# One convolution tap on ScalarE, the whole output projection in high and low parts, and a ring of three for modulation weights

## The chip, the cores and the metric

The kernel runs on one core of a Trainium2 chip. The metric is device time in microseconds (us) of one execution. Engines are named as in the profile: PE is TensorE (matmuls; PEld its weight loads), DVE is VectorE, ACT is ScalarE, POOL is GpSimd, SP is SyncE, which issues nearly all DMAs.

## What is computed

A trunk of two layers on one sequence of 256 tokens of width 1024. Each layer is a half-step SwiGLU feed-forward block (hidden width 2816), a token mixer, and another half-step feed-forward block. Every sublayer gets an RMS-normalized input with a shift and a scale, and its output a gate; these come from a conditioning vector through `mod_w` (a 1024 x 9216 matrix per layer). The mixer of layer 0 is stick-breaking attention, that of layer 1 the RG-LRU block, which the change is in:

```python
def rglru_block(h, w_in, conv_w, conv_b, w_r, b_r, w_i, b_i, lam, w_out):
    gate, xb = jnp.split(h @ w_in, 2, axis=-1)          # width 1280 each
    xp = jnp.pad(xb, ((0, 0), (CONV_W - 1, 0), (0, 0)))  # CONV_W = 4
    xc = conv_b + xp[:, 0:S] * conv_w[0]
    for tap in range(1, CONV_W):
        xc = xc + xp[:, tap:tap + S] * conv_w[tap]
    r = sigmoid(xblk @ w_r + b_r); i = sigmoid(xblk @ w_i + b_i)   # ten blocks of 128
    log_a = -LRU_C * r * softplus(-lam)
    a = exp(log_a); b = sqrt(-expm1(2 * log_a)) * (i * xc)
    hs = scan over tokens of  h = a * h + b
    return (gelu(gate) * hs) @ w_out
```

## The kernel before

Activations lie transposed, features on the 128 partitions and the 256 tokens along the free axis. A float32 product is made of three fp32r matmuls: weight and activation are each split into a high part (rounded to fp32r) and a low part (the rest), and high x high, high x low and low x high are summed in PSUM (`Acc.group`, the matmul is L553). A few products use a plain float32 matmul instead (`group32`, L570, and the gates' matmul, L1116), which needs no split.

Weights come in pieces of 128 x 2048 (1 MB) into a ring of three buffers (`raw`), by DMAs on SP's queue (`dma`, L495). `load` splits each piece in two halves of 1024 columns: ScalarE writes the high part (`wh`, L525), VectorE the low part (`wl`, L528), each into a ring of seven halves.

The modulation matrix is not multiplied on TensorE. `mod_tile` loads one tile of 128 x 1024 (512 KB) into a ring of four buffers (`rawm`), and VectorE multiplies it with the conditioning vector and sums it along the row (L585). There are 128 such tiles in this ring, handed out by `hook` between the steps of the feed-forward blocks and the attention, at a rate per step, each load ordered behind a matmul. The ring also holds three pieces of the weights of the RG-LRU's gates (`wg`).

Operations are collected with their buffers, and a planner (`Program.schedule`) puts them in an order per engine before the kernel is built, from its own costs, latencies and due times and from what is free in each ring. Each engine then runs its list in order, and semaphores make it wait where the other engines are later than planned. So a change of one ring or one operation can move other instructions too.

In the RG-LRU block (`rglru`) the branch `xb` is projected in five double tiles. Each tile n of 128 features is copied out of PSUM into a buffer of 4 + 256 columns by ScalarE, and `conv` makes the four taps on VectorE: a `tensor_scalar` with the weight of the first tap and the bias (L1095) and three `scalar_tensor_tensor` (L1098). `gates` makes two float32 matmuls (L1116), two sigmoids and a tanh on ScalarE, and a product (L1127). TensorE then does the five double tiles of the gate projection, while `decay` (exponentials and squares on ScalarE, L1173 on VectorE), `scan` (square root on ScalarE, L1179 and the scans L1182 on VectorE) and `output` (gelu on ScalarE, the product L1189 on VectorE) are made for the five double tiles. Exponential, square root and gelu each need another table on ScalarE, so all of a kind are made behind one table load (L1310).

`down` makes the output projection in five chunks c of two feature tiles, for eight output tiles d. In the first chunk (`N32 = 1`) the operand is the float32 product itself and the weights are the float32 piece, in sixteen plain float32 matmuls (L570). For the other four `output` splits the product: a copy on ScalarE is the high part, L1195 on VectorE the low part; and their weights are split by `load`. At the end of a `down` the residual (L695) follows for each d, then the square for the next norm and the scaled input of the next sublayer in two parts (`scaled`, L648), whose first matmuls start before the norm is known (`up_first`). `kick_op` (L740) is a small matmul that is put behind the first step of some chunks.

Of the kernel before, what the change touches and what calls it, by code (L numbers as in the profile page):

```python
# [10 lines left out]
AF = mybir.ActivationFunctionType  # L11
ALU = mybir.AluOpType
# [3 lines left out]
T = 256  # L16
TX = T + 2
D = 1024
# [4 lines left out]
NR = DR // P  # L23
# [21 lines left out]
OFF_CW = OFF_FG + KD  # L45
OFF_CB = OFF_CW + 4 * NR
# [306 lines left out]
def c_act(n, psum=False, ptr=0):  # L353
    return (51.0 if psum else 93.0) + 0.8333 * n + 93.0 * ptr


def c_dve(n):
    return 68.0 + 1.042 * n
# [11 lines left out]
def trunk(ctx, tc, xT, cb, par, modw, gu0, gu, wdn, qk, wv, wo, win, wri, wout, out):  # L370
    nc = tc.nc
    act, dve, pe, pool, sp = nc.scalar, nc.vector, nc.tensor, nc.gpsimd, nc.sync
# [10 lines left out]
    def ring(name, n, cols, dt=F32, pl=const, pitch=0):  # L383
        if pitch:
            whole = pl.tile([P, n * pitch], dt, tag=name, name=name)
            tiles = [whole[:, i * pitch : i * pitch + cols] for i in range(n)]
        else:
            tiles = [pl.tile([P, cols], dt, tag=f"{name}{i}", name=f"{name}{i}") for i in range(n)]
        return Space(name, n, lambda at, _: tiles[at]), tiles

    banks, _ = ring("bank", 8, 512, pl=psum)
    banks.exclusive = True
    rawr, _ = ring("raw", 3, CH)
    modr, _ = ring("rawm", 4, D)
    whr, _ = ring("wh", 7, HALF, F32R)
    wlr, _ = ring("wl", 7, HALF, F32R)
    const.tile([P, HXPAD], F32, tag="pad0", name="pad0")
    hxr, _ = ring("hx", 20, TX, F32R, pitch=320)
    const.tile([P, HKPAD], F32, tag="pad2", name="pad2")
    hkr, _ = ring("hk", 2, T, F32R)  # L400
    sqr, _ = ring("sq", 2, T)
    ssqr, _ = ring("ssq", 2, T)
    rmsr, _ = ring("rms", 1, T)
    rstr, _ = ring("rst", 1, T)
    hpr, _ = ring("hpre", 3, T)
    bcr, _ = ring("bc", 4, 2)
    tr, _ = ring("tr", 2, T)
    sgr, _ = ring("sg", 3, T)
# [6 lines left out]
    def new_phase(r_cells, f_cells, dts=(F32R, F32)):  # L415
        k = len(phases)
        prev = phases[-1]["spaces"] if phases else ()
        ph = {"size": (r_cells, f_cells), "dts": dts}

        def view(which):  # L420
            def v(at, n):
                enter(k)
                return phase["tiles"][which][:, at * CELL : (at + n) * CELL]
            return v

        ph["spaces"] = tuple(
            Space(f"ph{k}{n}", c, view(i), prev) for i, (n, c) in enumerate((("r", r_cells), ("f", f_cells))))
        phases.append(ph)
        return ph["spaces"]
# [15 lines left out]
    def fixed(name, cols, dt=F32):  # L445
        return const.tile([P, cols], dt, tag=name, name=name)
# [4 lines left out]
    pars = Buf(ap=fixed("pars", NPAR))  # L451
# [30 lines left out]
    def col(off, n=1):  # L482
        return pars()[:, off : off + n]
# [16 lines left out]
    def A(o, i, f, n, r, w, table=None, psum=False, ptr=0, after=(), **kw):  # L500
        def fn():
            act.activation(o(), i(), f, **{k: (v() if callable(v) else v) for k, v in kw.items()})  # L502
        return pr.op("ACT", c_act(n, psum, ptr), fn, r, w, after, table)

    def V(fn, n, r, w, cost=None, ptr=0):
        return pr.op("DVE", cost or c_dve(n) + 62.0 * ptr, fn, r, w)
# [572 lines left out]


    def rglru(l, s, nxt):
        N32 = 1
        R, F = new_phase(8 * (NB - N32), 86)
        xc, rr, th, gt, sig, wg, firsts = {}, {}, {}, {}, [], {}, []

        def of(t, n):
            return t[n // 2], n % 2, slice((n % 2) * T, (n % 2 + 1) * T)

        def conv(n, evict):
            xb = Buf(xbr)  # L1090
            evict(n % 2, xb)
            if n % 2 == 0:
                xc[n // 2] = Buf(F, 4)
            c, e, cs = of(xc, n)
            V(lambda: dve.tensor_scalar(c()[:, cs], xb()[:, 1 : 1 + T], col(OFF_CW + n), col(OFF_CB + n), ALU.mult,  # L1095
                                        ALU.add), T, [xb, pars], [(c, e)], ptr=2)
            for tap in range(1, 4):
                V(lambda tap=tap: dve.scalar_tensor_tensor(c()[:, cs], xb()[:, 1 + tap : 1 + tap + T],  # L1098
                                                           col(OFF_CW + tap * NR + n), c()[:, cs], ALU.mult, ALU.add), T,
                  [xb, pars, (c, e)], [(c, e)], ptr=1)  # L1100
# [28 lines left out]
        def xb_proj(n2):  # L1129
            if n2 == 0:  # L1130
                firsts.append(up_first((l, s), [load(win[1, i], CH, f"xb{i}") for i in range(NFIRST)]))
            if n2 < NFIRST:
                ts = next(firsts[0])

                def evict(e, xb):
                    t, rd, c = ts[e]
                    A(lambda: xb()[:, 4:], t, AF.Identity, T, [t, rd], [xb], ptr=1, bias=c)
            else:
                acc = Acc(f"xb{n2}")
                up(acc, load(win[1, n2], CH, f"xb{n2}"), (l, s), True)  # L1140

                def evict(e, xb):
                    A(lambda: xb()[:, 4:], lambda: acc.b()[:, e * T : (e + 1) * T], AF.Copy, T, [(acc.b, (e, 0))], [xb],
                      psum=True)
            for e in range(2):
                conv(2 * n2 + e, evict)
# [38 lines left out]
        def output(n2):  # L1185
# [3 lines left out]
            V(lambda: dve.tensor_tensor(t(), t(), g(), ALU.mult), 2 * T, tt + [g], tt)  # L1189
            if n2 < N32:  # L1190
                y = t
# [13 lines left out]
        for n2 in range(NB):  # L1205
            output(n2)
        down(l, s, nxt, [wout[:, 2 * c : 2 * c + 2, :].rearrange("p k d -> p (k d)") for c in range(NB)],
             lambda k: ys[k], 2, n32=N32, kicks=(N32,))

# [89 lines left out]
    ffn(0, 2, (1, 0), hook(2))  # L1299
    ffn(1, 0, (1, 1), hook(3))  # L1300
    rglru(1, 1, (1, 2))
    assert not todo
    ffn(1, 2, "end", lambda f: None)
# [62 lines left out]
```

## Time and profile before

| what | us |
|---|---|
| median of three runs (lowest, highest) | 962.55 (962.23, 963.67) |
| the profiled execution | 962.91 |
| its span, first to last instruction | 961.2 |
| TensorE busy in it | 949.2 |
| VectorE busy | 791.8 |
| ScalarE busy | 570.1 |
| the sixteen plain float32 products of the output projection (L570) | 7.2 |
| the first taps on VectorE (L1095, ten) | 4.1 |
| the modulation products in the ring (L585, 128) | 155.6 |

A line of a timeline has the start and the length in us, the engine, the line of the kernel, the operation, what it writes and reads, and in brackets the idle time before it and what ended that. A line of the groups has the count, the busy time in us, the mean ns of one and the idle time before. A line of a table by stretches has the stretch, then busy us and count for PE, PEld, DVE, ACT and POOL, then the granted clock of TensorE, the busy share of the DMA engines and GB/s. A line of waits has who waited for whom: us in total, times, longest us. A plain float32 matmul shows as two records.

### The profile page before, as it was taken

How to read it: one execution, taken by the hardware profiler on the slowest of the kernel's cores; microseconds unless marked ns; L12 is line 12 of the kernel's file. 1: busy time of each engine (PE TensorE's matmuls, PEld its weight loads, DVE VectorE, ACT ScalarE, POOL GpSimd, SP SyncE). 2: the span in 40 equal slices, each digit the busy share in tenths (PEclk: the TensorE clock that was granted, in tenths of full speed). 3: DMA queues.
4: the chain of work that ended last, by engine and by line, in shares of the span. 5: the costliest groups of instructions: out<-in, count | busy, mean ns of one | idle time of the engine just before them, and what ended most of it. 6: DMA issues, size and time to landing. Idle time of an engine off the chain costs nothing.

```text
span 961.2 us, 19726 instructions
## 1 busy us (share of the span) xinstructions
PE 949.2 (99%) x8132; PEld 936.2 (97%) x8132; DVE 791.8 (82%) x1291; ACT 570.1 (59%) x928; POOL 2.4 (0%) x15
## 2 busy tenths in 40 slices
PE   8999999999999999999999999999999999999996
PEld 6999999999999999999999999999999999999996
DVE  7899989798999999999799998855997996555443
ACT  6685544378886854454466545534879785445333
POOL 1000000000000000000000000000000000000000
PEclk9999999999999999999999999999999999999998
DMA  9979999945666489999976998965243746545531
GB/s 345 405 293 376 355 347 366 363 158 193 244 215 225 174 320 359 357 349 352 350 282 243 342 344 317 351 244 209 88 166 143 264 160 238 208 184 193 172 119 44
DMA packets 48044, 251.25 MB, mean 261 GB/s; under 512 B 5457, under 2 KB 6097, under 8 KB 28242
## 3 DMA queue, kind: packets, MB, share of 16 engines
q1 hardware_dynamic: 47378, 249.43, 69.8%
q8 instruction: 63, 1.03, 0.4%
q10 hardware_dynamic: 576, 0.56, 0.2%
q14 instruction: 27, 0.22, 0.1%
HBM read 248.92 MB, written 1.05 MB: 260 GB/s over the span
## 4 chain that ended last, share of the span: by engine, by line
PE 80%; DVE 8%; DMA 7%; ACT 3%; issue 2%; SPq 0%; DVEq 0%; ACTq 0%
PE bank L553 73%; DMA rawm<-in_modw 5%; DVE wl L528 2%; PE bank L919 2%; DVE arenaf L1098 1%; DMA raw<-in_gu 1%; PE bank L1042 1%; ACT arenaf L502 1%; PE bank L570 1%; ACT wh L525 1%; DVE rawm L585 1%; PE bank L630 1%; PE bank L995 1%; PE bank L1020 1%; DVE arenar L585 0%
## 5 line engine op out<-in xcount | busy, mean ns | idle before, releaser
L553 PE MATMUL bank<-hx,wh 128*128 128x256 f32 (+1 forms) x3236 | 560.5, 278 | 1.8 <-DVE hx L832 1.3
L525 ACT ACTIVATE wh<-raw 128x1024 fp32r<-128x1024 f32 (+1 forms) x328 | 336.2, 1046 | 282.1 <-PE bank L553 204.3
L553 PEld LDWEIGHTS bank<-hx,wh 128*128 128x128 f32 x3236 | 490.1, 188 | 3.8 <-DVE hx L832 1.8
L528 DVE TENSOR_TENSOR wl<-raw,wh 128x1024 fp32r<-128x1024 f32 (+1 forms) x328 | 389.2, 1208 | 105.4 <-ACT wh L525 104.9
L553 PE MATMUL bank<-hx,wl 128*128 128x256 f32 (+1 forms) x1618 | 448.0, 277 | 0.1
L553 PEld LDWEIGHTS bank<-hx,wl 128*128 128x128 f32 x1618 | 304.3, 188 | 0.3 <-DVE wl L528 0.3
L553 PE MATMUL bank<-arenar,wh 128*128 128x256 f32 x1664 | 285.0, 277 | 0.0
L553 PEld LDWEIGHTS bank<-arenar,wh 128*128 128x128 f32 x1664 | 250.6, 188 | 0.1
L553 PE MATMUL bank<-arenar,wl 128*128 128x256 f32 x832 | 229.7, 276 | 0.0
L585 DVE SCALAR_TENSOR_TENSOR rawm<-rawm,cact 128x1024 f32<-128x1024 f32 x128 | 155.6, 1220 | 20.8 <-DMA rawm<-in_modw 20.0
L553 PEld LDWEIGHTS bank<-arenar,wl 128*128 128x128 f32 x832 | 156.2, 188 | 0.0
L502 ACT ACTIVATE arenar<-a 128x256 fp32r<-128x256 f32 x88 | 35.4, 406 | 11.4 <-DVE a L773 10.8
L778 DVE TENSOR_TENSOR arenar<-a,arenar 128x256 fp32r<-128x256 f32 x88 | 36.4, 419 | 1.0 <-ACT arenar L502 1.0
L502 ACT ACTIVATE sg<-bank 128x256 f32<-128x256 f32 x82 | 29.8, 368 | 9.7 <-PE bank L553 9.7
L773 DVE TENSOR_TENSOR a<-bank,sg 128x256 f32<-128x256 f32 x82 | 34.1, 418 | 0.5 <-ACT sg L502 0.3
L553 PE MATMUL bank<-hk,wh 128*128 128x256 f32 x156 | 31.2, 291 | 0.0
L502 ACT ACTIVATE hx<-x,mf 128x256 fp32r<-128x256 f32 x40 | 18.5, 500 | 19.5 <-DVE x L695 19.5
L695 DVE SCALAR_TENSOR_TENSOR x<-bank,mf,x 128x256 f32<-128x256 f32 x48 | 21.6, 478 | 7.8 <-PE bank L553 7.7
L553 PEld LDWEIGHTS bank<-hk,wh 128*128 128x128 f32 x156 | 24.0, 188 | 0.5
L502 ACT ACTIVATE hx<-hpre,mf 128x256 fp32r<-128x256 f32 x41 | 19.9, 499 | 6.2 <-DVE hpre L656 5.4
L919 PE MATMUL bank<-wh,hx 128*128 128x256 f32 x128 | 23.4, 280 | 0.0
L502 ACT ACTIVATE arenaf<-arenaf 128x768 f32<-128x768 f32 (+1 forms) x31 | 22.0, 737 | 0.4
(115 smaller groups left out, 573.4 us busy)
## 6 DMA issues: line engine op xcount, KB each, us to landing
raw<-in_gu SPq DMA_DIRECT2D x79, 1024.0 KB, 6.0
rawm<-in_modw SPq DMA_DIRECT2D x128, 512.0 KB, 7.5
raw<-in_wdn SPq DMA_DIRECT2D x44, 1024.0 KB, 5.9
raw<-in_win SPq DMA_DIRECT2D x10, 1024.0 KB, 4.7
arenar<-in_modw SPq DMA_DIRECT2D x16, 512.0 KB, 9.7
raw<-in_qk SPq DMA_DIRECT2D x8, 1024.0 KB, 4.9
raw<-in_gu SPq DMA_DIRECT2D x14, 512.0 KB, 9.2
raw<-in_wout SPq DMA_DIRECT2D x5, 1024.0 KB, 5.2
```

What stands on the lines that cost most here:

```text
L502: act.activation(o(), i(), f, **{k: (v() if callable(v) else v) for k, v in kw.items()})
L525: act.activation(h()[:, :m], raw()[:, a : a + m], AF.Copy)
L528: dve.tensor_tensor(lo()[:, :m], raw()[:, a : a + m], f32(h()[:, :m]), ALU.subtract)
L553: pe.matmul(o(b()), wc(u()), xc(v()), start=start and n == 0, stop=stop and n == len(passes) - 1, skip_group_check=True)
L570: pr.op("PE", c_mm(n, 4), lambda: pe.matmul(o(b()), wc(w()), xc(x32()), start=start, stop=stop, skip_group_check=True), [w, x32] + ([] if ...
L585: dve.scalar_tensor_tensor(raw(), raw(), 1.0, cact(), ALU.mult, ALU.mult, accum_out=m()[:, t : t + 1])
L630: pr.op("PE", c_mm(T, 4), lambda i=i, q=q, c=c: pe.matmul(b()[:, :T], ones, q()[:, c], start=i == 0, stop=i == len(qs) - 1), [q] + [b] * ( ...
L695: dve.scalar_tensor_tensor(x[d](), acc.b()[:, j * T : (j + 1) * T], gate()[:, d : d + 1], x[d](), ALU.mult, ALU.add)
L773: V(lambda: dve.tensor_tensor(a(), b()[:, T:], sg(), ALU.mult), T, [(b, (1, 0)), sg], [a])
L778: V(lambda: dve.tensor_tensor(y[1](), a(), f32(y[0]()), ALU.subtract), n, [a, y[0]], [y[1]])
L919: pe.matmul(o, u()[:, tb * P : (tb + 1) * P], v()[:, c0 : c0 + 256], start=start and n == 0, stop=k == KD - 1 and n == 2, skip_group_check ...
L995: pe.matmul(zb[e]()[:, BL[i]], v()[rows, kc], w()[rows, qc], start=False, stop=i == 1 and n == 2, skip_group_check=True)
```

## The change

It has three parts. The convolution's tap of the token itself, with the bias, is made first, by one activation on ScalarE (scale and bias per partition) in place of the `tensor_scalar` on VectorE; the other three taps stay on VectorE. `N32` becomes 0, so that all five chunks of the output projection are split in high and low parts: the first chunk's weights too go through the `wh` and `wl` rings, its products are split by ScalarE and VectorE, and its `kick_op` stands in chunk 0 and not in chunk 1. The fp32r arena of this block grows from 32 to 40 cells of 128 columns. The ring `rawm` has three buffers in place of four.

```diff
-    modr, _ = ring("rawm", 4, D)
+    modr, _ = ring("rawm", 3, D)
...
     def rglru(l, s, nxt):
-        N32 = 1
+        N32 = 0
         R, F = new_phase(8 * (NB - N32), 86)
...
             c, e, cs = of(xc, n)
-            V(lambda: dve.tensor_scalar(c()[:, cs], xb()[:, 1 : 1 + T], col(OFF_CW + n), col(OFF_CB + n), ALU.mult,
-                                        ALU.add), T, [xb, pars], [(c, e)], ptr=2)
-            for tap in range(1, 4):
+            A(lambda: c()[:, cs], lambda: xb()[:, 4:], AF.Identity, T, [xb, pars], [(c, e)], ptr=2,
+              scale=lambda: col(OFF_CW + 3 * NR + n), bias=lambda: col(OFF_CB + n))
+            for tap in range(3):
                 V(lambda tap=tap: dve.scalar_tensor_tensor(c()[:, cs], xb()[:, 1 + tap : 1 + tap + T],
                                                            col(OFF_CW + tap * NR + n), c()[:, cs], ALU.mult, ALU.add), T,
                   [xb, pars, (c, e)], [(c, e)], ptr=1)
```

## The prediction

> **What bounds the kernel.** I read the page first: which engine is full, and whether it is full everywhere. Its part 1 and the slices of part 2:
>
> ```profile
> PE 949.2 (99%) x8132; PEld 936.2 (97%) x8132; DVE 791.8 (82%) x1291; ACT 570.1 (59%) x928; POOL 2.4 (0%) x15
> ...
> PE   8999999999999999999999999999999999999996
> ```
>
> TensorE (PE) is busy nearly everywhere, but a matmul that waits while it is pipelined also counts as busy. So I counted matmuls per stretch (busy us and count by engine, clock, DMA share): three long feed-forward stretches with modulation loads, and the first half of the RG-LRU.
>
> ```profile
> 72.00:192.00 120.00, 120.00 (x1060) 119.96 (x1059) 107.13 (x168) 56.89 (x85) 0.00 (x0) 1.00 0.95 362
> 336.00:480.00 144.00, 144.00 (x1271) 143.97 (x1270) 130.37 (x206) 69.55 (x106) 0.00 (x0) 1.00 0.93 348
> 528.00:624.00 96.00, 96.00 (x847) 95.96 (x847) 86.58 (x141) 49.03 (x78) 0.00 (x0) 1.00 0.91 339
> 689.00:726.40 37.40, 37.40 (x293) 36.35 (x293) 36.66 (x75) 29.40 (x59) 0.00 (x0) 1.00 0.45 166
> ```
>
> 120.00/1060, 144.00/1271 and 96.00/847 are all 0.113 us per matmul: one steady rate, at full clock, with the DMA engines at 0.91 to 0.95. TensorE's own work is the time there. The waits say how much cover it has:
>
> ```profile
> ACT wh L525 <- PE bank L553: 204.3, 113, 3.5
> ...
> DVE rawm L585 <- DMA rawm<-in_modw: 20.0, 21, 3.8
> ```
>
> What ScalarE waits for most, by far, is that TensorE frees a high part (113 times). So the splitting runs as far ahead as the ring of seven halves allows. A half feeds 24 matmuls, 2.7 us; seven are 19 us; less the half in use and the split, some 13 us are an estimate of the cover. The places where TensorE did lose time are in its timeline, at the seams of sublayers:
>
> ```profile
> 500.06 0.40 PE L553 MATMUL bank<-hx,wh 128*128 128x258 f32 x2
> ...
> 500.42 0.74 PE L553 MATMUL bank<-hx,wh 128*128 128x258 f32 x2
> ...
> 501.36 0.28 PE L553 MATMUL bank<-hx,wl 128*128 128x258 f32 x1
> 501.63 0.70 PE L630 MATMUL bank<-ssq,ones 128*128 128x256 f32 x2
> ```
>
> ```profile
> 741.62 0.28 PE L553 MATMUL bank<-hx,wl 128*128 128x256 f32 x1
> 742.23 7.17 PE L570 MATMUL bank<-arenaf,raw 128*128 128x256 f32 x32 [0.33 <-DVE arenaf L1189]
> 749.05 0.59 PE L553 MATMUL bank<-arenar,wh 128*128 128x256 f32 x2
> 749.47 0.28 PE L553 MATMUL bank<-arenar,wl 128*128 128x256 f32 x1
> ```
>
> At 500.42 a pair takes 0.74 for 0.40, and 501.36 to 501.63 is 0.27 for 0.12: 0.49 us lost. At 742.23 the output projection waits 0.33 for the first product of gate and scan (L1189).
>
> **The change part by part. Output projection.** The sixteen fp32 products run from 742.23 to 749.05; the next pair is 0.19 late (749.05 to 749.47, 0.42 for 0.23), so 7.0 us. Instead come 16 x 3 = 48 matmuls at 0.113, 5.4 us: **-1.6 us** of TensorE work.
>
> But the first chunk's operands now need a high and a low part. The prices, from the view of lines, and the order around them, from VectorE's timeline:
>
> ```profile
> L1195 DVE TENSOR_TENSOR arenar<-arenaf,arenar 128x512 fp32r<-128x512 f32 x4 | 2.7, 685 | 0.0
> L502 ACT ACTIVATE arenar<-arenaf 128x512 fp32r<-128x512 f32 x4 | 2.5, 628 | 1.9 <-DVE arenaf L1189 1.9
> ```
>
> ```profile
> 736.38 0.69 DVE L1179 TENSOR_TENSOR arenaf<-arenaf 128x512 f32<-128x512 f32 x1 [0.93 <-ACT arenaf L502]
> ...
> 741.50 0.67 DVE L1189 TENSOR_TENSOR arenaf<-arenaf 128x512 f32<-128x512 f32 x1
> 742.09 0.68 DVE L1182 TENSOR_TENSOR_SCAN arenaf<-arenaf 128x256 f32<-128x256 f32 x1
> 742.69 0.67 DVE L1179 TENSOR_TENSOR arenaf<-arenaf 128x512 f32<-128x512 f32 x1
> ```
>
> L1189 ends at 742.17. The high copy takes 0.63 on ScalarE (742.8). In the new order (the list of instructions of each engine in the changed kernel, which the planner fixes ahead of any run) VectorE does a scan and an L1179 before L1195, 0.60 each in sequence, so the low part starts at 743.3 and ends at 743.97. The second of the 48 matmuls needs it: it runs at about 744.03, as if the chunk had begun at 743.92 instead of 742.23. That is **+1.69 us**, and with the -1.6 above, +0.09.
>
> This holds if L1189 stays where it is, which ScalarE decides. Its timeline before that:
>
> ```profile
> 717.41 0.47 ACT L502 ACTIVATE arenaf<-bank,pars 128x256 f32<-128x256 f32 x1 [0.27 <-PE bank L1116]
> ...
> 726.40 1.28 ACT L1310 ACT_TABLE_LOAD   x1
> 727.69 4.11 ACT L502 ACTIVATE arenaf<-arenaf,nsp 128x256 f32<-128x256 f32 x10
> 731.71 2.70 ACT L502 ACTIVATE arenaf<-arenaf 128x512 f32<-128x512 f32 x5
> 734.42 1.28 ACT L1310 ACT_TABLE_LOAD   x1
> ```
>
> and the splits of weights between it, ahead of and behind it, by the view of lines with shapes apart:
>
> ```profile
> L528 DVE TENSOR_TENSOR wl<-raw,wh 128x1024 fp32r<-128x1024 f32 x320 | 384.0, 1221 | 105.4 <-ACT wh L525 104.9
> L525 ACT ACTIVATE wh<-raw 128x1024 fp32r<-128x1024 f32 x320 | 331.7, 1057 | 282.1 <-PE bank L553 204.3 <-issue 62.7 <-DMA raw<-in_gu 11.5
> ```
>
> **The tap.** VectorE loses ten tensor_scalars, ScalarE gains ten activations with two per-partition operands:
>
> ```profile
> L1095 DVE TENSOR_SCALAR arenaf<-xb,pars 128x256 f32<-128x256 f32 x10 | 4.1, 409 | 0.0
> L502 ACT ACTIVATE hx<-arenaf,mf,mf 128x256 fp32r<-128x256 f32 x7 | 4.2, 600 | 0.5 <-DVE arenaf L817 0.4
> ```
>
> So 4.1 us leave VectorE. On ScalarE it is 10 x 0.600 = 6.0 alone, 5.1 in sequence (instructions in sequence overlap by about 0.09: five of 0.63 in the 2.70 above; the splits take 0.96 and 1.13 so). In 689 to 726.4 VectorE has 0.7 us free of 37.4 and ScalarE 8.0, so the tap goes from the full engine into gaps. Bounds: nothing, and 6 us if every gap were needed. I take nothing, for ScalarE after the last gates is set by TensorE: from the first wait on them at 717.41 (717.6 with the switch below) the new order leaves four sigmoids from the bank and five `sg` at 0.36, four tanh at 0.40 and two splits at 0.96, 6.8 us, and the table load for the exponentials falls at 724.4, not 726.40. The old 9.0 held the same splits and waits for VectorE's L1127 besides. Two us are won.
>
> They are spent at once: the two high halves of the first output chunk stand in the new order between the squares and the load of the square-root table, 2 x 0.96 = 1.9 us. That load falls at 724.4 + 1.28 + 4.0 + 2.7 + 1.9 = 734.3, against 734.42. On VectorE the low halves (2 x 1.13) follow L1173 and end at 735.9, before the first square root (734.3 + 1.28 + 0.63 = 736.2). So L1179 starts at 736.3, not 736.38: **0**. Behind it, up to the last low part of the last chunk, VectorE has 14 instructions at 0.60 and 8 splits at 1.13, 17.4 us from 743.3, ending at 760.8; TensorE needs it after 144 + 7 matmuls, 17.1 us from 743.92, at 761.0. **0**, with a margin of 0.2; the bounds are 0 and 0.5.
>
> [...]
>
> One product pair of the gates moves ahead of the last six matmuls of a projection: a second change from fp32 to fp32r, **+0.19** by the 749.05 row.
>
> **Ring of three.** Loads and VectorE's product per tile:
>
> ```profile
> rawm<-in_modw SPq DMA_DIRECT2D x128, 512.0 KB, 7.5
> ```
>
> ```profile
> L585 DVE SCALAR_TENSOR_TENSOR rawm<-rawm,cact 128x1024 f32<-128x1024 f32 x128 | 155.6, 1220 | 20.8 <-DMA rawm<-in_modw 20.0
> ```
>
> A slot is held 7.5 + 1.2 us and whatever VectorE makes it wait. In the densest stage three tiles go with two weight loads (96 matmuls, 10.9 us), so three slots suffice while a slot turns round within 10.9 us; four gave 14.5. A load issued late holds up what stands behind it on SP, the next weight load, and VectorE waits in order at L585 with the splits behind it. Both have the 13 us of cover. No load is added or made larger. I cost the ring at **0**; bounds 0 and +5.5 (below). One gain comes with the new order: before the loss at 500.42, a product of a tile and a split are taken out of VectorE's way:
>
> ```profile
> 495.19 1.22 DVE L585 SCALAR_TENSOR_TENSOR rawm<-rawm,cact 128x1024 f32<-128x1024 f32 x1
> ```
>
> That one moves to after the seam, and a split goes behind the last L648. The operand that TensorE waited for comes 1 to 2 us sooner: **-0.49**; bounds 0 and -0.49.
>
> **The sum:** +0.09 + 0 + 0.19 + 0 - 0.49 = -0.2 us. The profiled execution took 962.91 (span 961.2 and 1.7 around it), which gives 962.7. That execution was 0.36 above the median of 962.55, so I forecast **962.3**.
>
> **Rivals.** *ScalarE late (slower).* If the ten activations delay the chain, and ScalarE comes to the last gates after TensorE has made them, each us of that goes to L1189 and to TensorE's wait. It decides once fewer than 5.1 of ScalarE's 8.0 free us can be used where they lie. Losing the lead of 2.0 and 1 us more gives 965.3. For it: copy, tap and VectorE's three taps follow each other per tile. Against: VectorE's 4.1 us come back to the same chain. Chance 0.15. [...]
>
> *Ring starves (slower).* If a slot turns round in 12.2 us, each 10.9 us of the dense stages lose 1.3: 14, 17 and 11 us, less 13 of cover each, +5.5: 967.8. For it: VectorE already waits 20.0 us for these tiles. Against: the cover. Chance 0.07.
>
> *No new wait at the projection (faster).* If the lead of 2 us did reach L1189, -1.6, the old 0.5 between 741.73 and 742.23, -0.49 and +0.19 give 960.1. Against it stand the two splits ahead of the table load. Chance 0.10.
>
> **How the numbers follow.** Forecast 0.68. About 0.2% (1.9 us) is what a measurement of this kernel can tell from no change. Faster by more: most of the last rival, 0.08. Slower by more: the ring and most of ScalarE late, 0.20. Within: 0.72. The range 959.9 to 965.4 takes in the faster rival and leaves out the ring, the worse half of ScalarE late and a little at each end: 0.18.
>
> **What would show it.** L570 gone and 48 more L553; a wait of some 1.5 to 2.5 us before the projection's first low part; the exponentials' table load 2 us sooner after the last gates; no loss at the seam near 500; still 0.113 us per matmul in the dense stretches. Wrong would be a dense stretch with fewer matmuls (ring), or a wait over 3 us at the projection (ScalarE).

## The result and the profile after

The changed kernel takes 964.53 us (median of 17 runs, 962.57 to 966.69), against 962.43 (961.82 to 964.02, 17 runs) for the kernel before on the same chip: a ratio of 1.0020, 95% interval 1.0014 to 1.0026. It is slower by 2.1 us. That lies inside the range on record, but the forecast, 962.3, was a small gain. The runs of the changed kernel spread over 4.1 us instead of 2.2. The execution traced first took 963.17 (span 961.3), one of its shorter ones; a third trace, of a later execution, took 965.54 (span 963.8). That spread is part of the answer.

From the page of the changed kernel, and from its waits (what waits, for what: us in total, times, longest), the lines that answer to those of before. Lines from 1098 on stand one lower than before:

```profile
PE 948.5 (99%) x8148; PEld 936.2 (97%) x8148; DVE 791.9 (82%) x1284; ACT 576.8 (60%) x941; POOL 2.4 (0%) x15
...
rawm<-in_modw SPq DMA_DIRECT2D x128, 512.0 KB, 6.6
```

```profile
DVE rawm L585 <- DMA rawm<-in_modw: 28.7, 30, 2.6
```

```profile
SPq L495 <- DVE rawm L585: 161.3, 72, 7.5
```

and the last of them in the kernel before:

```profile
SPq L495 <- DVE rawm L585: 67.5, 27, 7.4
```

Here the ring is at work: the queue that issues loads waits for a product of a modulation tile to free a slot, 161.3 us for 67.5. VectorE waits more often for a tile, 30 times for 21. The dense stretches of the changed kernel (columns as before: TensorE's busy us and count, then the other engines; granted clock; DMA share):

```profile
72.00:192.00 120.00, 120.00 (x1060) 119.96 (x1059) 105.29 (x165) 56.06 (x83) 0.00 (x0) 1.00 0.94 349
336.00:480.00 144.00, 144.00 (x1271) 143.97 (x1271) 131.43 (x207) 69.41 (x105) 0.00 (x0) 1.00 0.95 353
528.00:624.00 96.00, 96.00 (x848) 95.96 (x847) 86.33 (x142) 48.48 (x79) 0.00 (x0) 1.00 0.90 334
```

They hold as many matmuls as before, 0.113 us each. So nothing is lost in the stretches. At the output projection, TensorE, ScalarE and VectorE in the same execution:

```profile
741.45 0.28 PE L553 MATMUL bank<-hx,wl 128*128 128x256 f32 x1
742.78 0.39 PE L553 MATMUL bank<-arenar,wh 128*128 128x256 f32 x1 [1.05 <-ACT arenar L502]
743.90 0.39 PE L553 MATMUL bank<-arenar,wh 128*128 128x256 f32 x1 [0.73 <-DVE arenar L1196]
744.13 0.28 PE L553 MATMUL bank<-arenar,wl 128*128 128x256 f32 x1
```

```profile
724.38 1.28 ACT L1311 ACT_TABLE_LOAD   x1
...
734.32 1.28 ACT L1311 ACT_TABLE_LOAD   x1
```

```profile
741.39 0.67 DVE L1190 TENSOR_TENSOR arenaf<-arenaf 128x512 f32<-128x512 f32 x1
...
743.16 0.68 DVE L1196 TENSOR_TENSOR arenar<-arenaf,arenar 128x512 fp32r<-128x512 f32 x1
...
760.21 0.69 DVE L1196 TENSOR_TENSOR arenar<-arenaf,arenar 128x512 fp32r<-128x512 f32 x1
```

One matmul starts in the 2.45 us from 741.45 to 743.90; this is the wait that the prediction worked out, at nearly the time that it gave.

### The profile page after: what moved, and what is told of

The parts are those of the page before. It is cut to its first block, busy times and chain, and to the rows that moved or that the text cites. A ratio compares the mean times of both kernels' runs of the same rounds, so it can differ in the third digit from the quotient of the medians.

```text
span 961.3 us, 19823 instructions
## 1 busy us (share of the span) xinstructions
PE 948.5 (99%) x8148; PEld 936.2 (97%) x8148; DVE 791.9 (82%) x1284; ACT 576.8 (60%) x941; POOL 2.4 (0%) x15
## 4 chain that ended last, share of the span: by engine, by line
PE 83%; DVE 6%; DMA 6%; ACT 3%; issue 2%; SPq 0%; DVEq 0%; ACTq 0%
PE bank L553 77%; DMA rawm<-in_modw 5%; PE bank L919 2%; DVE wl L528 2%; DVE rawm L585 1%; ACT arenaf L502 1%; PE bank L1042 1%; PE bank L630 1%; PE bank L995 1%; PE bank L1020 1%; ACT wh L525 1%; PE bank L1117 1%; DMA x<-in_xT 0%; DVE x L695 0%; DVE arenar L585 0%
## 5 line engine op out<-in xcount | busy, mean ns | idle before, releaser
L553 PE MATMUL bank<-hx,wh 128*128 128x256 f32 (+1 forms) x3236 | 560.2, 278 | 1.1 <-DVE hx L832 0.7
L553 PEld LDWEIGHTS bank<-hx,wh 128*128 128x128 f32 x3236 | 490.0, 188 | 2.5 <-DVE hx L832 1.2
L553 PE MATMUL bank<-hx,wl 128*128 128x256 f32 (+1 forms) x1618 | 448.0, 277 | 0.1
L553 PEld LDWEIGHTS bank<-hx,wl 128*128 128x128 f32 x1618 | 304.3, 188 | 0.3 <-DVE wl L528 0.3
L553 PE MATMUL bank<-arenar,wh 128*128 128x256 f32 x1696 | 290.6, 277 | 1.8 <-ACT arenar L502 1.1
L553 PEld LDWEIGHTS bank<-arenar,wh 128*128 128x128 f32 x1696 | 255.5, 188 | 2.3 <-ACT arenar L502 1.3
L553 PE MATMUL bank<-arenar,wl 128*128 128x256 f32 x848 | 234.2, 276 | 0.0
L585 DVE SCALAR_TENSOR_TENSOR rawm<-rawm,cact 128x1024 f32<-128x1024 f32 x128 | 155.9, 1220 | 29.4 <-DMA rawm<-in_modw 28.7
L553 PEld LDWEIGHTS bank<-arenar,wl 128*128 128x128 f32 x848 | 159.2, 188 | 0.0
L553 PE MATMUL bank<-hk,wh 128*128 128x256 f32 x156 | 31.1, 291 | 0.0
L553 PEld LDWEIGHTS bank<-hk,wh 128*128 128x128 f32 x156 | 24.0, 188 | 0.5
```

The source lines that it names most:

```text
L553: pe.matmul(o(b()), wc(u()), xc(v()), start=start and n == 0, stop=stop and n == len(passes) - 1, skip_group_check=True)
L585: dve.scalar_tensor_tensor(raw(), raw(), 1.0, cact(), ALU.mult, ALU.mult, accum_out=m()[:, t : t + 1])
```

## The experiments

All matmuls of two traces can be laid side by side. Where the distance between the same matmuls grows, one trace lost time against the other. In all 20 traces of this study the distance changes in only four places: the first 50 us, 195 to 214, 495 to 516 (both seams between sublayers), and 690 to 790. Everywhere else the traces agree within 0.03 us. Four theories were put against this. **T1**: the ring of three costs the time, at seams. **T2**: the changes in the RG-LRU cost it. **TC**: TensorE's own quiet before the output projection halves its clock for a while. **TR**: long executions are long by the ring alone. (T3: only parts together; T4: slow loads in the stretches; T5: everything a little; TO: slow operands behind the wait.)

What was timed, each beside runs of the kernel before on the same chip. A ratio's interval that contains 1 says that the two can't be told apart.

| Kernel | median (range), runs | before | ratio, 95% interval |
|---|---|---|---|
| ring of three alone | 963.26 (961.66–965.07), 11 | 962.32 | 1.0010, 1.0001–1.0018 |
| the same again | 962.67 (961.95–966.40), 12 | 962.18 | 1.0011, 1.0001–1.0021 |
| order of three, four buffers | 962.14 (962.01–964.51), 11 | 962.32 | 1.0002, 0.9993–1.0010 |
| tap alone | 962.51 (961.16–963.11), 11 | 962.32 | 0.9999, 0.9990–1.0008 |
| projection alone | 966.52 (966.47–966.88), 6 | 962.19 | 1.0040, 1.0026–1.0054 |
| the same, zeros in the wait | 964.52 (963.64–965.95), 9 | 962.18 | 1.0020, 1.0011–1.0030 |
| changed, ring of four | 963.59 (961.94–966.43), 11 | 962.32 | 1.0016, 1.0006–1.0026 |
| the same, zeros in the wait | 962.42 (961.77–964.12), 11 | 962.18 | 1.0002, 0.9993–1.0010 |
| changed (ring of three), zeros in the wait | 963.40 (962.08–967.48), 11 | 962.18 | 1.0017, 1.0005–1.0028 |
| changed, ring of four, high parts first | 962.49 (961.80–964.20), 11 | 962.27 | 1.0004, 0.9995–1.0013 |
| the same, order of three, four buffers | 962.51 (961.74–965.18), 11 | 962.27 | 1.0005, 0.9996–1.0014 |

### One part at a time

The ring of three alone is the kernel before with one edit:

```diff
-    modr, _ = ring("rawm", 4, D)
+    modr, _ = ring("rawm", 3, D)
```

> The kernel before with the ring of modulation tiles cut from four to three, and nothing else. T1 (the ring costs the 2 us: VectorE waits in its order for tiles that land late, and at the seams between sublayers nothing covers that): 964.0 to 965.0, with a spread of 3 us or more over its runs and 27 us or more of VectorE waiting for rawm at L585. T2 (the changes in the RG-LRU cost it): 961.5 to 962.6, a spread near 2 us, and no loss at 202. T3 (no part alone, only together, for instance by where the buffers lie): under 963.2.

It is slower by 0.94 us, less than T1 named, with a spread of 3.4 us and 26.9 us of VectorE waiting for tiles. That is T1 in kind, not in size. The ring in the same planned order, but over four buffers taken in turn:

```diff
-    modr, _ = ring("rawm", 4, D)
+    modr, modt = ring("rawm", 4, D)
+    modr = Space("rawm", 3, lambda at, n: None)      # planned as three
...
+        turn[-1].space_tile = modt[(len(turn) - 1) % 4]   # run on four
```

> The same order of instructions as with the ring of three, but four buffers behind it, taken in turn, so that a load need not wait for the product three tiles before it. T1 with the slots at run time as the mechanism: back to 961.5 to 962.6, VectorE's waits for rawm at 22 us or less. T1 with the planned order as the mechanism (loads are planned later and VectorE's products stand elsewhere): like the ring of three, 964 to 965, and the waits stay near 28. T2: as before, 962.4.

It can't be told from before. So as far as these runs can tell the order is not at fault, and the slots at run time are. The wait of the load queue on that ring, in its trace (where L505 and L595 are L495 and L585):

```profile
SPq L505 <- DVE rawm L595: 18.8, 10, 4.0
```

That is 18.8 us, against 160.1 in the trace of the ring of three alone. The other side of the comparison, the changed kernel with its ring put back to four:

```diff
-    modr, _ = ring("rawm", 3, D)
+    modr, _ = ring("rawm", 4, D)
...
-        R, F = new_phase(8 * (NB - N32), 86)
+        R, F = new_phase(8 * (NB - N32), 83)
```

> The changed kernel with the ring put back to four (the RG-LRU's arena is three cells of 512 bytes smaller to make room; the order of the RG-LRU is that of the changed kernel). T1: 962.2 to 963.0 (the projection's +0.09 and the switch's +0.19 on the kernel before, and the loss at 500 stays), spread near 2 us. T2: 964 to 965, like the changed kernel. T3: between, 963.0 to 964.0.

963.59: by this neither theory alone is right. Its runs fall into two heaps, four of 961.9 to 962.3 and seven of 963.6 to 966.4. The tap alone, the diff of `conv` only:

> The kernel before with the own-token tap and bias on ScalarE, ring of four, first output chunk still in fp32. T1: 961.8 to 962.8 (2 us of lead for ScalarE at the last gates, at most the 0.33 before the projection gained, 0.19 for the switch lost). T2 with the tap as the culprit: 964 or more, with the wait ahead of the projection at 742 grown by 1.5 us or more. T3: under 963.2.

No difference that can be told, as T1 said. In its trace the wait before the projection is gone, and 0.4 us is lost again near 783; between 741 and 790 it gains 0.17.

The projection alone (`N32 = 0` in the kernel before, ring of four, arena 83):

> The kernel before with all of the output projection in high and low parts, ring of four, tap still on VectorE (the RG-LRU's arena three cells smaller to make room). Of the +1.3 of the changed kernel with a ring of four: T2a (the projection alone brings it, with a spread of 4 us): 963.2 to 964.2, some runs near 962.2 and some over 964.5. T2b (it takes the tap as well, which moves ScalarE's chain): 962.0 to 962.8, spread near 2 us. By the wait for the first low part alone, which no lead of 2 us softens here, and no high halves ahead of the square roots' table load: 962.3 to 963.5.

All six runs lie between 966.5 and 966.9, above all of these expectations. With the tap still on VectorE there is no lead of 2 us, and TensorE's wait is longer, 741.30 to 745.57. But a longer wait isn't all. Its trace in steps of 2 us (after the other engines' columns the granted clock, the DMA share, GB/s):

```profile
744.00:746.00 2.00, 0.81 (x5) 0.57 (x5) 2.00 (x4) 2.00 (x4) 0.00 (x0) 1.00 0.00 0
746.00:748.00 2.00, 2.00 (x12) 2.00 (x12) 2.00 (x4) 2.00 (x4) 0.00 (x0) 0.56 0.00 0
748.00:750.00 2.00, 2.00 (x13) 2.00 (x12) 2.00 (x3) 2.00 (x3) 0.00 (x0) 0.59 0.08 16
```

PE is busy for all of the 2.00 us of both last rows, but with 12 and 13 matmuls, where such a row shows 20 at the full rate (the last row of the next such table), and the clock stands at 0.56 and 0.59. This is TC: nobody makes TensorE wait there, it runs at half rate, behind its own quiet.

### Longer executions traced

The same two kernels again, for traces of longer executions:

> The changed kernel with a ring of four once more, for a trace of one of its longer executions (11 runs lay between 961.9 and 966.4). If the time is over 963.4: T2 (the RG-LRU's margins) has the extra time at TensorE's waits between 742 and 775; T4 (the loads of the weights, in the feed-forward stretches) has it in a stretch with fewer matmuls than 0.113 us each allows; T5 (all through) has it nowhere in particular. If under 963.4: as in the first trace of it.

> The same kernel a third time, for the same purpose: over 963.4 the extra time is in one place by T2 (742 to 775), in a feed-forward stretch by T4, spread by T5.

> The changed kernel again, for a second trace (its 17 runs lay between 962.6 and 966.7, the one traced at 963.2). T1: a longer execution has more at the seams near 202, 320 and 500, behind VectorE's waits for rawm. T2: it has the extra time between 742 and 775. T4: in a feed-forward stretch.

> The changed kernel a third time, for a trace of a long execution. TC: over 964.5, the products behind the wait at 742 to 744 run at half rate for about 3.6 us and lose about 1.6; under 963.9, the clock is 1.00 there and the rest lies at the start and at the seam near 202. TR (a rival: long executions are long by the ring alone): over 964.5 with the clock at 1.00, and over 2 us lost at the seams.

> The changed kernel a fourth time, for the same purpose: over 964.5 with half rate behind the wait by TC, with clock 1.00 by TR.

They took 965.15, 962.58, 963.79, 965.54 and 962.89. The two over 965 show the half rate; the other three, and the two earlier traces of these kernels, show a clock of 1.00. The third trace of the changed kernel itself, 965.54, in steps and by TensorE's rows:

```profile
742.00:744.00 2.00, 0.52 (x2) 0.32 (x3) 2.00 (x5) 1.94 (x3) 0.00 (x0) 1.00 0.00 0
744.00:746.00 2.00, 2.00 (x11) 1.96 (x12) 2.00 (x3) 2.00 (x4) 0.00 (x0) 0.56 0.00 0
746.00:748.00 2.00, 2.00 (x13) 2.00 (x13) 2.00 (x4) 2.00 (x4) 0.00 (x0) 0.59 0.00 0
748.00:750.00 2.00, 2.00 (x20) 2.00 (x19) 2.00 (x3) 2.00 (x5) 0.00 (x0) 1.00 0.82 225
```

```profile
744.26 0.78 PE L553 MATMUL bank<-arenar,wh 128*128 128x256 f32 x2
...
746.97 0.63 PE L553 MATMUL bank<-arenar,wh 128*128 128x256 f32 x2
747.39 0.40 PE L553 MATMUL bank<-arenar,wl 128*128 128x256 f32 x1
747.61 0.43 PE L553 MATMUL bank<-arenar,wh 128*128 128x256 f32 x2
747.87 0.28 PE L553 MATMUL bank<-arenar,wl 128*128 128x256 f32 x1
```

Three matmuls take 0.64 us (746.97 to 747.61) instead of 0.34. That costs 1.5 us by 748, against the first trace. The other trace, of the kernel with a ring of four, runs at half rate from 745.76 to 749.18 (its rows from 744 to 750 stand at 0.94, 0.50 and 0.71) and loses 1.6. TR falls for this execution: it lost 0.74 at the seam near 202 and nothing at 500.

In each of the three traces with the half rate it lasts about 3.4 us (an estimate from the rows: 0.56 and 0.59 of 2.00 us here and in the projection alone, 0.94, 0.50 and 0.71 in the execution of 965.15, taken as times at 0.50 and at 1.00). What tells these executions from the shorter ones doesn't show in the rows. In the first trace of the changed kernel the wait lies where it does in the execution of 965.54, 741.45 to 743.90 against 741.45 to 743.86, and TensorE is busy for nearly as much of the two rows with the wait, 1.73 and 0.48 us against 1.72 and 0.52; yet the clock stays at 1.00 behind it:

```profile
742.00:744.00 2.00, 0.48 (x2) 0.28 (x2) 2.00 (x5) 1.90 (x3) 0.00 (x0) 1.00 0.00 0
744.00:746.00 2.00, 2.00 (x18) 1.95 (x19) 2.00 (x3) 2.00 (x4) 0.00 (x0) 1.00 0.00 0
746.00:748.00 2.00, 2.00 (x20) 2.00 (x19) 2.00 (x4) 2.00 (x4) 0.00 (x0) 1.00 0.03 8
```

So the half rate follows the wait of 2.45 us in 2 of 7 traces, and why in these two isn't shown. The wait of 4.27 us has 3.61 us of idle time in its one trace, which shows the half rate; all six runs of the projection alone lie between 966.47 and 966.88.

### The quiet filled

If the quiet of TensorE does it, work that adds nothing must undo it. Multiplications with a block of zeros go into the wait, as many as fit:

```diff
                 for n, i in enumerate(passes):
+                    for _ in range(fill[n] if n < 2 else 0):
+                        pe.matmul(o(b()), zero[:, :P], zero, start=n == 0, stop=False, skip_group_check=True)
                     u, v = seq[i]
```

Nothing else in the order changes. `fill` is (26, 8) for the projection alone, (10, 8) for the others, and only ahead of the first product of this projection.

> The projection-alone kernel (966.5, matmuls at half rate from 746.15 to 749.81, right behind a wait of 4.3 us at 741.30), with matmuls that multiply zeros in TensorE's wait: 26 ahead of the first product and 8 ahead of the second, of about 0.113 us each, so that they end before the operands come. They add nothing to the result. TC (the quiet of TensorE itself halves its clock for a while afterwards): granted clock 1.00 from 744 to 752, the 48 products at 0.113 us, and 1.8 us less, 964.5 to 965.0. TO (the products are slow because their operands come slowly, or because VectorE and ScalarE crowd memory): no change, 966.4 to 966.9, and the granted clock still near 0.56.

The median is 964.52, 2.0 us less, as TC said; between the two traces the gain behind the wait is 1.6. TensorE's rows in it (L558 is L553 there, L556 the zeros), and its steps:

```profile
741.91 3.01 PE L556 MATMUL bank<-zero 128*128 128x256 bf16 x26
744.95 0.38 PE L558 MATMUL bank<-arenar,wh 128*128 128x256 f32 x1
745.17 1.05 PE L556 MATMUL bank<-zero 128*128 128x256 bf16 x8
746.07 0.39 PE L558 MATMUL bank<-arenar,wh 128*128 128x256 f32 x1
```

```profile
746.00:748.00 2.00, 2.00 (x18) 1.89 (x17) 2.00 (x4) 2.00 (x4) 0.00 (x0) 1.00 0.04 8
748.00:750.00 2.00, 2.00 (x20) 2.00 (x19) 2.00 (x4) 2.00 (x3) 0.00 (x0) 1.00 0.00 0
```

There are 18 and 20 matmuls for 12 and 13, with ScalarE and VectorE as busy as without the zeros: TO falls too.

> The changed kernel (ring of three) with such matmuls in its wait of 2.45 us: 10 ahead of the first product and 8 ahead of the second. TC: the wait halves the clock in some executions and not in others; without that the median falls from 964.5 to 962.9 to 963.5, and the runs over 965 go. TO: no change, 964.0 to 965.0 with runs over 966. T1 for what is left (ring of three): 0.5 to 1.0 above the kernel before, by the seam near 202.

> The changed kernel with a ring of four and the same 18 matmuls in the wait. TC: 962.0 to 962.6, most runs within 0.6 us of each other, none over 964.5 (a late seam near 202 can still add 1.3). TO: as without them, a median near 963.6 and some runs over 965. If the ring costs nothing of its own, this and the filled kernel with a ring of three come out within 0.3 us.

The medians are 963.40 and 962.42. With a ring of four the upper heap is gone: nine of eleven runs lie between 961.8 and 962.6, two at 964.1. With a ring of three the median falls by what was expected, but by their ratios the kernels with and without zeros (1.0005 to 1.0028, 1.0014 to 1.0026) can't be told apart. Two runs with zeros lie at 966.8 and 967.5, which TC had excluded; they weren't traced. The ring of three alone, which has no such wait, has two untraced runs at 966.3 and 966.4. The two kernels of this pair differ by the ring, and in their medians by 1.0 us.

Instead of zeros, the quiet can be shortened with useful products: in the first output chunk all that need only the high part of the gated scan go first.

```diff
-                        step(d, k)
+                        step(d, k, (0, 2) if first else (0, 1, 2))
...
+                        step(d, k, (1,))      # after all of these, the low parts
```

> The changed kernel with a ring of four, and the products of the first output chunk in another order: all 32 that need only the high part of the gated scan first, then the 16 that need its low part. TensorE's quiet falls from 2.4 to 1.3 us (to the high copy at 742.07 in the trace of that kernel). TC: the clock stays at 1.00; the last chunk's low part, behind a full VectorE until 760, takes most of the earlier start back, so 961.5 to 962.5 with few runs over 963.5. If the wait's length did not matter: as the kernel with a ring of four, a median near 963.6.

> High parts first as in e15, and the order of the ring of three with four buffers behind it: without both causes. If the two are all there is: 961.3 to 962.3, a spread near 2 us, clock 1.00 behind the wait, no loss at 500 and seldom one at 202. If something else is left: over 962.6. It is also the version that could beat both kernels, by 0.3 to 0.9 us.

They take 962.49 and 962.51, with the clock at 1.00 in the trace of each: TensorE's quiet in the trace of the first is 1.30 us, 742.77 to 744.07, for 2.45, and in these runs the shorter quiet does what zeros do. Neither beats the kernel before. Why the earlier start isn't a gain shows in TensorE's rows of the first:

```profile
744.07 0.38 PE L553 MATMUL bank<-arenar,wh 128*128 128x256 f32 x1 [1.03 <-ACT arenar L502]
...
762.25 0.38 PE L553 MATMUL bank<-arenar,wh 128*128 128x256 f32 x1 [0.64 <-DVE arenar L1204]
```

The wait for the first low part has moved to the last chunk's low part (L1204 there), behind a VectorE that is full there (busy for 1.90 us or more of each 2.00 from 742 to 762). The second takes away both causes. It lies between its two answers, and can't be told from the kernel before: the two causes account for the loss as far as can be measured, but there is nothing to win behind them.

### The ring and the seams

> The kernel before with only the ring of three, again, for more runs and a second trace (11 runs before had a median of 963.26, between 961.7 and 965.1). T1 (its slots make loads and VectorE's products late at the seams): 963.0 to 963.6, clock 1.00 throughout, and in a trace of over 963.2 the extra time at the seams near 202, 320 or 500. If the ring costs nothing: 962.0 to 962.6.

> The ring of three alone, for a trace of a long execution (23 runs lay between 961.7 and 966.4). T1: what is over 961.9 lies at the seam near 202 (VectorE's last product before it waits for its tile until later than about 186.5, and each us of that is lost), and in a run over 964 also at another seam. If it lies in the first 50 us, the ring's late loads are not what makes the long runs.

> The same kernel a fourth time, for the same purpose: by T1 the extra time over 961.9 is at the seam near 202 and in long runs at a second one; else in the first 50 us or in no one place.

They took 962.67 in the median (traced at 962.96), 964.02 and 964.66. In its median the ring alone costs 0.5 here, under T1's 963.0; the ratio, 1.0011, is that of the first time. The two long executions lose most of their time at the seams. VectorE near 187, in the first traces of before and of the changed kernel:

```profile
183.91 1.22 DVE L585 SCALAR_TENSOR_TENSOR rawm<-rawm,cact 128x1024 f32<-128x1024 f32 x1
...
187.07 2.36 DVE L528 TENSOR_TENSOR wl<-raw,wh 128x1024 fp32r<-128x1024 f32 x2 [1.94 <-ACT wh L525]
189.35 0.87 DVE L695 SCALAR_TENSOR_TENSOR x<-bank,mf,x 128x256 f32<-128x256 f32 x2
```

```profile
187.10 1.23 DVE L585 SCALAR_TENSOR_TENSOR rawm<-rawm,cact 128x1024 f32<-128x1024 f32 x1 [1.24 <-DMA rawm<-in_modw]
...
188.25 2.36 DVE L528 TENSOR_TENSOR wl<-raw,wh 128x1024 fp32r<-128x1024 f32 x2
190.52 0.87 DVE L695 SCALAR_TENSOR_TENSOR x<-bank,mf,x 128x256 f32<-128x256 f32 x2
```

Before, the tile's product is done while VectorE would wait anyway. Now the tile lands at 187.1; the two splits and the residual behind it come 1.17 later, and so do the scaled inputs of the next sublayer at the end of that chain. TensorE, at the seam of the changed kernel:

```profile
201.68 0.28 PE L553 MATMUL bank<-hx,wh 128*128 128x258 f32 x1
202.39 0.38 PE L553 MATMUL bank<-hx,wh 128*128 128x258 f32 x1 [0.42 <-DVE hx L648]
```

Call t the time at which this product of a tile starts, less the shift with which TensorE came out of the first 50 us. In all eleven traces that lose time at this seam the loss is t - 186.5, within 0.02; in the nine others t is under 186.5 and the loss is 0.00. For example, the fourth trace of the ring alone (shift 0.03, loss 1.50), and the third, where the seam near 202 loses nothing but the one near 500 loses 1.42:

```profile
188.03 1.23 DVE L585 SCALAR_TENSOR_TENSOR rawm<-rawm,cact 128x1024 f32<-128x1024 f32 x1 [1.78 <-DMA rawm<-in_modw]
```

```profile
487.51 1.22 DVE L585 SCALAR_TENSOR_TENSOR rawm<-rawm,cact 128x1024 f32<-128x1024 f32 x1 [2.28 <-DMA rawm<-in_modw]
```

By traces: with three buffers the seam near 202 lost time in 7 of 9 (0.2 to 1.5 us), with four in 3 of 11 (1.0 to 2.0; a fourth by 0.02); the one near 500 in 2 of 9 (1.0 and 1.4), and in 3 of 11 (0.2 to 0.8). So the loss is not new with the ring. In these traces the ring makes it the rule near 202, where it was the exception; near 500 the counts are too alike to say so.

## Why the prediction was wrong

The time lies inside the range, but not for a reason that the prediction gave: neither of the two causes below is in its sum, and none of its rivals came true.

**What held.** The working of the RG-LRU came out nearly to the tenth. Predicted and traced: exponentials' table load 724.4 and 724.38, square roots' 734.3 and 734.32, first low part 743.3 and 743.16, second of the 48 matmuls 744.03 and 743.90, last low part ready 760.8 and 760.90. Projection and switch to fp32r were put at +0.09 and +0.19; where the clock stayed up, the traces show +0.22 to +0.27 between 741 and 790. The tap alone, put at 0, is 0.19 us above before in its median and can't be told from it (0.9990 to 1.0008). The lead of 2 us that the prediction gave the tap is there, and it is spent at the projection, as the prediction said: without the tap the wait is 4.27 us instead of 2.45, and the two kernels with zeros and a ring of four take 964.52 without it and 962.42 with it. With both causes below taken away, the kernel takes 962.42 against 962.18.

**The new wait at the projection: the step failed in what follows the wait.** It was priced by its length alone, +1.69, and that length was right. What it does to the products behind it wasn't priced: the 48 matmuls were put at 0.113 us each. In 2 of 7 traces with this wait some 16 of them run at half rate, which costs 1.5 to 1.6 us. In the projection alone, whose wait is 4.27, zeros won 2.0 us in the median. For the changed kernel, against its own runs of before, zeros bring +2.1 to +1.2 with a ring of three, and +1.3 to +0.2 with four: 0.9 to 1.0 us of the 2.1. The size is uncertain: 2 of 7 at 1.6 us would be 0.5 us in the mean (an estimate from the traces), and with a ring of three the two intervals overlap.

The trace of the kernel before gives no sign of it at the projection: the rows from 736 to 754 stand at 1.00 there, and TensorE's wait for the first product is 0.33 us. The question belonged on the wait that the change makes. A quiet of 2.45 us with one matmul in it was enough at times, one of 4.27 in its one trace; behind one of 1.30 the clock stayed at 1.00. What decides among the executions with 2.45 isn't shown, so these traces name no length of wait that is safe.

**The ring of three, put at 0: the step failed.** "Both have the 13 us of cover" holds for the splits of weights, and the dense stretches bear it out. It doesn't hold for VectorE at the end of a sublayer: behind its last products of tiles stand the residuals and the scaled inputs of the next sublayer, which have no ring in front of them, and TensorE waits for them at once. In the first trace of the changed kernel VectorE waits 1.24 us for a tile there, and TensorE loses 1.1. The medians give 0.9 and 0.5 for the ring alone, and 1.0 between the two kernels with zeros. The rival "ring starves" had the right sign at the wrong place: it expected dense stretches with fewer matmuls.

**The gain at 500, put at -0.49, was no gain of the order.** The loss of 0.49 that the prediction read there (0.78 over the whole seam) was an accident of the one execution of before that was traced. Six of the eight other traces with an unchanged order at this seam have none. So "no loss at the seam near 500" came true in the changed kernel's first trace by luck, and two traces with the new order do lose time there. The prediction also took off 0.36 because that execution was longer than the median, and so counted part of one accident twice. A stall of under 1 us in one trace should have been traced twice before it was put into a sum.

The sum by what was measured, in us: +0.2 for projection, tap and switch (962.42 against 962.18), +1.0 for the clock (with a ring of four), +1.0 for the ring (with zeros). That is 2.2, and 2.1 were measured. The terms are differences of the same medians (with the clock's 0.9 of a ring of three they must add up to 2.1), so the sum shows only that the clock costs about as much with either ring.

## What to carry to other kernels

A wait of TensorE had two prices here: its length, and the half rate behind it (1.5 to 1.6 us, in 2 of 7 traces of the wait of 2.45 us). So look at the granted clock of the rows behind every new wait of such a length, in several executions, and fill or shorten the wait (zeros won 2.0 us here in the longest). Count a ring's cover separately for each consumer: an engine that works in order carries a late buffer into everything behind it (1.17 us on VectorE near 187), and what lies at a seam has no cover (TensorE lost 1.1 near 202). And where a kernel's runs spread more than before, trace a long one too: the half rate was in none of the shorter ones.

## What was not expected of the hardware

In the execution of 965.54 the clock is back at 1.00 from 748, but TensorE stays a little slower until 774. One row of it, and the same one of the first trace of the changed kernel:

```profile
754.00:760.00 6.00, 6.00 (x53) 6.00 (x52) 5.89 (x7) 4.17 (x5) 0.00 (x0) 1.00 0.40 137
```

```profile
754.00:760.00 6.00, 6.00 (x55) 6.00 (x54) 5.90 (x7) 4.49 (x5) 0.00 (x0) 1.00 0.40 132
```

There are 53 matmuls for 55, 0.118 us from start to start for 0.113; that costs 1.0 more by 774. The other two traces with the half rate don't show it. What decides it stays open.
